# Low parts of keys and compressed probabilities as products over 128 partitions, and conditioning sums further down TensorE's list

## The chip, the cores and the metric

The kernel runs on one core of a Trainium2 chip. The metric is device time in microseconds (us) of one execution. Engines: PE is TensorE (products; PEld is its weight load), DVE is VectorE, ACT is ScalarE, POOL is GpSimd, SP is SyncE, which issues the DMAs here.

## What is computed

One decoder layer for 512 tokens of width 1024, in float32, with a conditioning vector `c`:

```
mod = (silu(c) @ w_ada + b_ada).reshape(9, 1024)            # shifts, scales, gates
x = x + 0.5 * gt1 * swiglu(modulate(rmsnorm(x, g1), sh1, sc1))
x = x + gt2 * mixer(modulate(rmsnorm(x, gm), sh2, sc2))
x = x + 0.5 * gt3 * swiglu(modulate(rmsnorm(x, g2), sh3, sc3))
out = rmsnorm(x, g_final)
```

The mixer projects its input once, into a gated depthwise convolution and into attention: 8 query heads of 64, in 2 groups that share keys and values. Each head has three branches, whose outputs are gated and added: over compressed blocks of keys (31 of them), over selected blocks, and over a window of 512. With 512 tokens the selected blocks and the window hold all earlier tokens. Both groups' outputs are normed and projected.

## The kernel before

Activations lie transposed, channels on partitions, tokens along the free axis. Products run in fp32r. To keep the precision of float32 an operand is split into a high part (rounded by ACT) and a low part (the difference, by DVE or POOL), and a product is made of three: `mm3` is high by high, high by low, low by high. Weights stream in units of 128x1024 (`raw`), are split into `whi` and `wlo`, and are freed when PE has used them.

The kernel is written as tasks (Python generators) that ask a planner (`Plan`) for an engine, with a cost in us. The planner places them in order of rank and of its own estimates of time; what comes out is one fixed list of instructions per engine. On the chip each engine follows its list in order and waits for what an instruction needs. `go(rank, task)` starts a task; `Slots` are buffers that tasks take and give back; `Event` is a point that tasks wait for. Names in the trace are those of the tiles: `b` is a PSUM bank, `hhi`, `hlo` the normed input, `ghi`, `glo` the gated values of the feed-forward part.

The order in time: the first feed-forward part with the first modulation (to some 410 us), beside which the other seven rows of `mod` are made; the mixer's first group of projections (to 470), the rest of the projections mixed with attention (to 665), the output projection, the second feed-forward part (from 706).

**Conditioning sums.** `ada_loads` brings `w_ada` in 56 loads of 512 KB through three buffers (`araw`); `ada_sums` adds eight of them, each scaled by its part of `silu(c)`, into `ada` on DVE (two such tiles). When the eighth is in, `ada_reduce` adds over partitions by PE (4 products with a matrix of ones), copies, transposes and adds the bias.

**Scores.** For head pair `c`, branch `b` (selected blocks, window) and group `s`, `scores` makes four tiles of 128 tokens by 128 to 512 keys, in three PSUM banks. Its `q` holds 128 rows: for group 0 the high part of the query in the lower 64 and the low part in the upper 64, for group 1 the other way round. `kst[b][s]` (in the trace `ks`) holds the high part of the keys in both halves, so that one product over 128 rows gives high by high and low by high. The third, the query's high part by the keys' low part, is a product over the 64 rows where the high part lies; `klo[b]` (`kl`) holds group 0 in its lower and group 1 in its upper half:

```
mm(a, q[:, tt], st[:, :w], True, False)
mm(a, q[hs, tt], lo[hs, :w], False, True)
```

The planner's cost for these is 2 * max(w / 2370, 0.105) us at a width of w. After that come the mask and a minimum (DVE, `P`), the exponential (ACT), a scaling, transposes on PE (line 1407), a split into `PT` and the products with the values (`values`: 128 columns of output for the high part of `PT`, 64 for its low part, in the same bank).

**Compressed branch.** `compressed` leaves the transposed probabilities as high part `pcs[0]` and low part `pcs[1]` of 64 rows (both groups' 32 blocks), and `values` ends each head with a product of 64 rows by 64 columns and one of 64 rows by 128 (`pc,vcs`). The upper half of that bank (the values' low parts) is copied to `low` and added later by `pair`.

Of the kernel before, what the change touches and what calls it, by code (L numbers as in the profile page):

```python
# [10 lines left out]
F32 = mybir.dt.float32  # L11
F32R = mybir.dt.float32r
BF16 = mybir.dt.bfloat16
I32 = mybir.dt.int32
AF = mybir.ActivationFunctionType
# [4 lines left out]
P = 128  # L20
T = 512
D = 1024
DK = D // P
# [4 lines left out]
HD = 64  # L28
# [45 lines left out]
A_ACT = 3  # L74
HOLD = 0
N_AW = 3
KEEP = (2, 2, 0)
N_PT = 4
R_H0 = 0.4
# [56 lines left out]
class Plan:  # L136
# [12 lines left out]
    def go(self, rank, task):  # L149
        self.n += 1  # L150
        self.step([rank, self.n, task, [self.at], None], None)
# [67 lines left out]
def c_act(n):  # L219
    return ACT, 0.1 + 0.84e-3 * n  # L220
# [18 lines left out]
def c_pts(n):  # L239
    return POOL, 0.26 + 0.83e-3 * n  # L240
# [15 lines left out]
def tile_hymba_layer(ctx: ExitStack, tc: tile.TileContext, xT, pos, cols_d, con_d, wa0, wa1, f1a, f1b, f1d,  # L256
                     wia, wib, wiv, wc1, woa, wob, f2a, f2b, f2d, out):
    nc = tc.nc
# [25 lines left out]
    def mm(o, lhsT, rhs, start, stop):  # L284
        nc.tensor.matmul(o, lhsT, rhs, start=start, stop=stop)  # L285
# [576 lines left out]
            done(aw_in[n])  # L862

    def ada_sums():
        for n in range(7 * DK):
            i, k = divmod(n, DK)
            yield aw_in[n]
            if k == 0:
                j = yield adas
            a, w = ada[j], aw[aw_at[n]]  # L870
            if k == 0:
                yield c_ts(D)
                nc.vector.tensor_scalar(a, w, cact[:, 0:1], None, op0=OP.mult)
            else:
                yield c_stt(D)
                nc.vector.scalar_tensor_tensor(a, w, cact[:, k:k + 1], a, op0=OP.mult, op1=OP.add)  # L876
            give(aws, aw_at[n])
            if k == DK - 1:
                go(R_ADA, ada_reduce(order[i], j))

    def ada_reduce(m, j):

# [90 lines left out]
    with ExitStack() as mixer:  # L973
# [6 lines left out]
        G = mx.tile([P, NB, 24], F32, name="G")  # L980
        valid = kv("valid").rearrange("p (t n) -> p t n", t=NB)
        vneg = mx.tile([P, NB, 32], F32, name="vneg")
        vcs = [mx.tile([64, P], F32R, name=f"vcs{g}") for g in range(2)]
        kcs = [mx.tile([P, 64], F32R, name=f"kcs{g}") for g in range(2)]
        ecmp = mx.tile([P, NB, 2, 32], F32, name="ecmp")
        kst = [[mx.tile([P, T], F32R, name=f"ks{b}{g}") for g in range(2)] for b in range(2)]
        klo = [mx.tile([P, T], F32R, name=f"kl{b}") for b in range(2)]
        q_of = [[mx.tile([P, T], F32R, name=f"q{i}{g}") for g in range(2)] for i in range(2)]
        p_of = [[mx.tile([P, (t + 1) * P], F32, name=f"P{i}{t}") for i in range(N_P[t])] for t in range(NB)]
        ps_ = [Slots(range(n)) for n in N_P]  # L990
# [13 lines left out]
        def constants():  # L1004
            for s_ in swp_of:
                yield c_pts(T)
                nc.gpsimd.memset(s_, 0.0)
            yield c_pts(P)
            nc.gpsimd.tensor_scalar(vneg, valid, 1.0, NEG, op0=OP.subtract, op1=OP.mult)
            yield c_pts(P)  # L1010
            for g in range(2):
                nc.gpsimd.memset(vcs[g].bitcast(F32), 0.0)
            for g in range(2):
                yield c_pts(64)
                nc.gpsimd.memset(kcs[g].bitcast(F32), 0.0)
            yield c_pts(64)
            nc.gpsimd.memset(blk[:, :, :, NC_CMP:], 0.0)
            done(ready0)
# [61 lines left out]
        def keys(b):  # L1080

            def then(o):
                for g, h in enumerate((LO_, HI_)):
                    for part in ((LO_, HI_) if g == 0 else (HI_, LO_)):
                        yield from copy(kst[b][g][part], o[h], T)
                    yield c_tt(T)
                    nc.vector.tensor_sub(klo[b][h], o[h], kst[b][g][h].bitcast(F32))
                done(k_in[b])
            return then

# [55 lines left out]
        def compressed_keys(bs):  # L1146
# [31 lines left out]
            for g in range(2):  # L1178
                r = slice(g * 32, (g + 1) * 32)
                yield ACT, 0.2  # L1180
                nc.scalar.activation(vcs[g][r, LO_], pt[r, :HD], AF.Copy)
                yield SMALL
                nc.vector.tensor_sub(vcs[g][r, HI_], pt[r, :HD], vcs[g][r, LO_].bitcast(F32))
            done(vc_in)
            side_free(ib)
            ib = yield from side_bank()
# [18 lines left out]
        def compressed(c):  # L1205
# [46 lines left out]
                nc.tensor.transpose(pt[:64, t * P:(t + 1) * P], e[:, t].rearrange("p a b -> p (a b)"), ident)  # L1252
            give(e_free, 0)
            yield c_act(T)
            nc.scalar.activation(pcs[0], pt[LO_], AF.Copy)
            yield c_tt(T)
            nc.vector.tensor_sub(pcs[1], pt[LO_], pcs[0].bitcast(F32))
            side_free(ib)
            done(pc_in[c])

        pc_turn = [Event() for _ in range(5)]
        e_free, pc_free = Slots([0]), Slots([0])
        pcs = [mx.tile([HD, T], F32R, name=f"pc{i}") for i in range(2)]

        low, lows = mx.tile([P, T], F32, name="low"), [Slots([0]), Slots([0])]
        pc_in, cq_done = [Event() for _ in range(4)], [Event() for _ in range(4)]
        z_in, z_of = [Event() for _ in range(8)], {}

# [47 lines left out]
        def scores(c, b, s, n_, order):  # L1316
# [1 line left out]
            yield begun[n_]  # L1318
            yield k_in[b]
            yield q_in[c]  # L1320
            hs = (LO_, HI_)[s]
            q, st, lo = q_of[q_at[c]][s], kst[b][s], klo[b]
            k = yield hsmall
            m, su = small_of[k][:, 0, :, 0], small_of[k][:, 1, :, 0]
            pi, left = None, [NB]
# [18 lines left out]
            for ts in ((3,), (2,), (1, 0)):  # L1344
                j = yield caps["s"]
                bk = yield banks
                if ts[-1] == 0:
                    done(begun[n_ + 1])
                yield PE, sum(2 * max((t + 1) * P / 2370, 0.105) for t in ts)
                at = 0  # L1350
                a_of = {}
                for t in ts:
                    w = (t + 1) * P
                    tt = slice(t * P, w)
                    a_of[t] = a = bank_of[bk][:, at:at + w]
                    at += w
                    mm(a, q[:, tt], st[:, :w], True, False)
                    mm(a, q[hs, tt], lo[hs, :w], False, True)
                n = [len(ts)]

                def free(n=n, j=j, bk=bk):
                    n[0] -= 1
                    if not n[0]:
                        give(caps["s"], j)
                        give(banks, bk)

                for t in ts:
                    go(order, softmax(t, a_of[t], free))
# [59 lines left out]
        def values(c, s):  # L1428
# [17 lines left out]
            yield pc_in[c]  # L1446
            yield vc_in
            yield PE, 0.43
            mm(o[LO_], vcs[s][:, LO_], pcs[1], False, False)
            mm(o, vcs[s], pcs[0], False, True)  # L1450
            summed[c] += 1
            if summed[c] == 2:
                give(pc_free, 0)
            yield lows[s]
            yield c_act(T)
            nc.scalar.activation(low[(LO_, HI_)[s]], o[HI_], AF.Copy)
            yield zp_open
            y = z_tile[4 + c]
            yield c_act(T)
            nc.scalar.activation(y[(LO_, HI_)[s]], o[LO_], AF.Copy)  # L1460
# [4 lines left out]
        def pair(c):  # L1465
            for s in range(2):
                yield attended[c][s]
            y = z_tile[4 + c]
            e = yield c_tt(T), (*c_ptt(T), POOL_TAX)
            (nc.vector if e == DVE else nc.gpsimd).tensor_add(y, y, low)  # L1470
            for s in range(2):
                give(lows[s], 0)
            yield from group_norm(y, cv("ga", c), 4 + c)

        summed = [0] * 4
        zp_open, z_tile = Event(), {0: mx.tile([P, T], F32, name="z0")}

        def free_queries(c):
# [147 lines left out]
        plan.run(early_done)  # L1626
        early.close()
        zp = mixer.enter_context(tc.tile_pool(name="zp", bufs=1))
        for k in range(1, 8):
            z_tile[k] = zp.tile([P, T], F32, name=f"z{k}")  # L1630
        for i in range(N_LATE_P):
# [272 lines left out]
```

## Time and profile before

| | us |
|---|---|
| median of 3 runs | 1070.98 (1069.9 to 1071.71) |
| the profiled execution | 1075.31 |
| its span in the trace | 1073.5 |
| PE busy | 1048.8 |
| DVE busy | 607.3 |
| ACT busy | 409.2 |
| POOL busy | 50.1 |

The trace is of one execution. An engine is busy while it runs an instruction; a matmul's end is modelled, and the next may start before it, so that PE's pace is better read from the starts of its products. The view of one stretch after another tells which engine is full where.

### The profile page before, as it was taken

Reading aid. Unit: us, or ns where it says so; the run is one execution under the profiler, and the core shown is the slowest. Engines: PE = TensorE matmul, PEld = TensorE weight load, DVE = VectorE, ACT = ScalarE, POOL = GpSimd, SP = SyncE. Lnnn points to the kernel's source line nnn. Section 1 sums busy time; section 2 is a strip of 40 time slices with the busy share of each in tenths; the row PEclk is TensorE's granted clock in tenths of the full one; section 3 lists DMA queues with packets and bytes.
Section 4 is the critical chain, followed back from the end, with each engine's and each line's share of the span. In section 5 each row is a group of like instructions: output and inputs, shape, how many; then the busy total and the mean of one; then the engine's idle time right before and its main releaser. Section 6 shows DMA issues by size and latency. Waiting matters only on the chain.

```text
span 1073.5 us, 13889 instructions
## 1 busy us (share of the span) xinstructions
PE 1048.8 (98%) x5417; PEld 865.9 (81%) x5417; DVE 607.3 (57%) x1069; ACT 409.2 (38%) x713; POOL 50.1 (5%) x47
## 2 busy tenths in 40 slices
PE   8899999999999999999999999999999999999997
PEld 5787777788888889987777677898888888888887
DVE  4978788833333347499788687664333333333334
ACT  4542222122222233347756685444222112222321
POOL 0310000000000001012001010100000000000000
PEclk8899999999999999999999899999999999999998
DMA  9659889522232230343300002314333322333302
GB/s 340 253 194 323 310 310 318 183 98 98 98 98 98 98 103 16 131 126 120 132 25 28 13 13 78 112 60 137 98 96 94 94 95 95 97 98 98 99 20 79
DMA packets 40707, 133.60 MB, mean 124 GB/s; under 512 B 4705, under 2 KB 8033, under 8 KB 40001
## 3 DMA queue, kind: packets, MB, share of 16 engines
q1 hardware_dynamic: 40640, 132.71, 36.7%
q8 instruction: 42, 0.69, 0.3%
q14 instruction: 25, 0.20, 0.1%
HBM read 130.14 MB, written 2.10 MB: 123 GB/s over the span
## 4 chain that ended last, share of the span: by engine, by line
PE 80%; DVE 9%; DMA 7%; issue 2%; ACT 1%; SPq 0%; DVEq 0%; ACTq 0%
PE b L285 77%; DMA araw<-in_wa_dram 6%; DVE ada L876 3%; PE b L1407 2%; DVE wlo L366 1%; DVE s L530 0%; ACT whi L377 0%; DVE afirst L747 0%; DMA raw<-in_f1b_dram 0%; DMA x<-in_xT_dram 0%; DVE s L611 0%; DVE glo L618 0%; PE b L1302 0%; DVE s L1050 0%; DVE swp L1053 0%
## 5 line engine op out<-in xcount | busy, mean ns | idle before, releaser
L285 PE MATMUL b<-hhi,whi 128*128 128x512 f32 (+1 forms) x1020 | 383.7, 376 | 1.1 <-ACT hhi L534 1.1
L285 PE MATMUL b<-hlo,whi 128*128 128x512 f32 (+1 forms) x1020 | 376.6, 369 | 0.7 <-DVE hlo L536 0.7
L285 PE MATMUL b<-hhi,wlo 128*128 128x512 f32 (+1 forms) x1020 | 376.5, 369 | 0.0
L377 ACT ACTIVATE whi<-raw 128x1024 fp32r<-128x1024 f32 (+3 forms) x176 | 178.0, 1012 | 445.0 <-PE b L285 300.7
L366 DVE TENSOR_TENSOR wlo<-raw,whi 128x1024 fp32r<-128x1024 f32 (+3 forms) x162 | 191.0, 1180 | 213.5 <-ACT whi L377 212.4
L285 PEld LDWEIGHTS b<-hhi,whi 128*128 128x128 f32 x1020 | 193.5, 190 | 38.9 <-issue 6.5
L285 PEld LDWEIGHTS b<-hhi,wlo 128*128 128x128 f32 x1020 | 193.6, 190 | 32.2
L285 PEld LDWEIGHTS b<-hlo,whi 128*128 128x128 f32 x1020 | 193.7, 190 | 30.4 <-DVE hlo L536 1.0
L285 PE MATMUL b<-ghi,whi 128*128 128x512 f32 (+1 forms) x364 | 136.4, 375 | 0.0
L285 PE MATMUL b<-ghi,wlo 128*128 128x512 f32 (+1 forms) x364 | 135.7, 373 | 0.0
L285 PE MATMUL b<-glo,whi 128*128 128x512 f32 (+1 forms) x364 | 135.7, 373 | 0.0
L611 DVE TENSOR_TENSOR s<-sg,b 128x512 f32<-128x512 f32 x44 | 30.1, 685 | 101.9 <-PE b L285 101.2
L285 PEld LDWEIGHTS b<-ghi,whi 128*128 128x128 f32 x364 | 68.5, 188 | 12.8 <-issue 0.8
L285 PEld LDWEIGHTS b<-ghi,wlo 128*128 128x128 f32 x364 | 68.5, 188 | 12.1
L285 PEld LDWEIGHTS b<-glo,whi 128*128 128x128 f32 x364 | 68.5, 188 | 12.0
L876 DVE SCALAR_TENSOR_TENSOR ada<-araw,cact,ada 128x1024 f32<-128x1024 f32 x49 | 66.6, 1360 | 18.9 <-DMA araw<-in_wa_dram 18.4
L543 DVE SCALAR_TENSOR_TENSOR x<-b,mod,x 128x512 f32<-128x512 f32 (+1 forms) x30 | 19.1, 643 | 41.0 <-PE b L285 40.9
L366 POOL TENSOR_TENSOR wlo<-raw,whi 128x768 fp32r<-128x768 f32 (+2 forms) x14 | 31.1, 2220 | 216.6 <-ACT whi L377 216.6
L461 ACT ACTIVATE s<-x 128x256 f32<-128x256 f32 (+1 forms) x41 | 19.4, 491 | 55.4 <-DVE x L543 53.6
L616 ACT ACTIVATE ghi<-s 128x512 fp32r<-128x512 f32 x44 | 27.5, 630 | 22.3 <-DVE s L611 22.3
L534 ACT ACTIVATE hhi<-s,mod 128x256 fp32r<-128x256 f32 (+1 forms) x42 | 20.9, 534 | 29.4 <-DVE s L530 26.3
L1416 ACT ACTIVATE PT<-b 128x384 fp32r<-128x384 f32 (+1 forms) x48 | 24.5, 524 | 17.9 <-PE b L1407 17.3
(238 smaller groups left out, 974.3 us busy)
## 6 DMA issues: line engine op xcount, KB each, us to landing
araw<-in_wa_dram SPq DMA_DIRECT2D x56, 512.0 KB
raw<-in_f1b_dram SPq DMA_DIRECT2D x38, 512.0 KB
raw<-in_f2b_dram SPq DMA_DIRECT2D x38, 512.0 KB
raw<-in_f1d_dram SPq DMA_DIRECT2D x22, 512.0 KB
raw<-in_f2d_dram SPq DMA_DIRECT2D x22, 512.0 KB
raw<-in_wib_dram SPq DMA_DIRECT2D x14, 512.0 KB
wfirst<-in_wa_dram SPq DMA_DIRECT2D x5, 1024.0 KB
raw<-in_wc_dram SPq DMA_DIRECT2D x8, 512.0 KB
```

Source lines behind the costliest of these rows:

```text
L285: nc.tensor.matmul(o, lhsT, rhs, start=start, stop=stop)
L366: (nc.vector if e == DVE else nc.gpsimd).tensor_sub(wlo_of[j][:, :n], raw_of[i][:, :n], whi_of[j][:, :n].bitcast(F32))
L377: nc.scalar.activation(whi_of[j][:, :n], raw_of[raw_at[u]][:, :n], AF.Copy)
L461: nc.scalar.activation(o[:, ts], x[d][:, ts], AF.Square)
L534: nc.scalar.activation(hhi[d][:, ts], t, AF.Identity, bias=sh)
L543: nc.vector.scalar_tensor_tensor(x[d][:, ts], bank_of[b][:, ts], gate, x[d][:, ts], op0=OP.mult, op1=OP.add)
L611: nc.vector.tensor_mul(scr_of[q], sg_of[k], bank_of[bu])
L616: nc.scalar.activation(ghi[j], scr_of[q], AF.Copy)
L876: nc.vector.scalar_tensor_tensor(a, w, cact[:, k:k + 1], a, op0=OP.mult, op1=OP.add)
L1407: nc.tensor.transpose(pt[:, w:w + P], Pr[t][:, kb * P:(kb + 1) * P], ident)
L1416: nc.scalar.activation(ph[:, :w], pt[:, :w], AF.Copy)
```

## The change

- `klo` gets a tile for each branch and group, as `kst` has. Its other half is set to zero by POOL when the mixer begins (four memsets of 64x512), and the product of the low part runs over all 128 rows of `q`: the zeros take the query's low part out.
- `pcs` becomes one tile of 128 rows, high part below, low part above. `vcs` gets 128 rows; ACT copies the values' high part a second time, beside the low part of `pcs`. One product over 128 rows takes the place of two over 64.
- `low` moves into the pool `zp`, which is opened later (`zp_open`); the wait for it stands ahead of the copy to `low` and no longer behind it.
- `ada_sums` calls `ada_reduce` when the fourth load of the next eight is added (`LATER = 3`), and no longer at once; the last of the seven at once, as before.

```
+LATER = 3
...
     def ada_sums():
+        summed = []
         for n in range(7 * DK):
...
             if k == DK - 1:
-                go(R_ADA, ada_reduce(order[i], j))
+                summed.append((order[i], j))
+            if summed and (k == LATER or n == 7 * DK - 1):
+                go(R_ADA, ada_reduce(*summed.pop()))
...
-        vcs = [mx.tile([64, P], F32R, name=f"vcs{g}") for g in range(2)]
+        vcs = [mx.tile([P, P], F32R, name=f"vcs{g}") for g in range(2)]
...
-        klo = [mx.tile([P, T], F32R, name=f"kl{b}") for b in range(2)]
+        klo = [[mx.tile([P, T], F32R, name=f"kl{b}{g}") for g in range(2)] for b in range(2)]
...
+            for b in range(2):
+                for g, other in enumerate((HI_, LO_)):
+                    yield c_pts(T)
+                    nc.gpsimd.memset(klo[b][g][other].bitcast(F32), 0.0)
...
-                    nc.vector.tensor_sub(klo[b][h], o[h], kst[b][g][h].bitcast(F32))
+                    nc.vector.tensor_sub(klo[b][g][h], o[h], kst[b][g][h].bitcast(F32))
...
+                yield ACT, 0.2
+                nc.scalar.activation(vcs[g][HD + g * 32:HD + (g + 1) * 32, LO_], pt[r, :HD], AF.Copy)
...
-            nc.scalar.activation(pcs[0], pt[LO_], AF.Copy)
+            nc.scalar.activation(pcs[LO_], pt[LO_], AF.Copy)
             yield c_tt(T)
-            nc.vector.tensor_sub(pcs[1], pt[LO_], pcs[0].bitcast(F32))
+            nc.vector.tensor_sub(pcs[HI_], pt[LO_], pcs[LO_].bitcast(F32))
...
-            hs = (LO_, HI_)[s]
-            q, st, lo = q_of[q_at[c]][s], kst[b][s], klo[b]
+            q, st, lo = q_of[q_at[c]][s], kst[b][s], klo[b][s]
...
-                    mm(a, q[hs, tt], lo[hs, :w], False, True)
+                    mm(a, q[:, tt], lo[:, :w], False, True)
...
-            mm(o[LO_], vcs[s][:, LO_], pcs[1], False, False)
-            mm(o, vcs[s], pcs[0], False, True)
+            mm(o, vcs[s], pcs, False, True)
...
             yield lows[s]
+            yield zp_open
             yield c_act(T)
-            nc.scalar.activation(low[(LO_, HI_)[s]], o[HI_], AF.Copy)
-            yield zp_open
+            nc.scalar.activation(low_of[0][(LO_, HI_)[s]], o[HI_], AF.Copy)
```

What the planner makes of it is seen in the engines' lists. PE, at the first of the seven sums over partitions (`ada,con`), before, among the projections of the first feed-forward part (rows 429 to 433 of its list):

```order
L285 MATMUL b_64<-hlo_121,whi_100 128x512
L285 MATMUL b_64<-hhi_113,wlo_101 128x512
L285 MATMUL b_70<-ada_663,con 32x256 x4
L285 MATMUL b_64<-hhi_114,whi_100 128x512
L285 MATMUL b_64<-hlo_122,whi_100 128x512
```

and the same sum now, at rows 465 to 469:

```order
L286 MATMUL b_65<-hlo_117,whi_96 128x512
L286 MATMUL b_65<-hhi_109,wlo_97 128x512
L286 MATMUL b_66<-ada_663,con 32x256 x4
L286 MATMUL b_65<-hhi_110,whi_96 128x512
L286 MATMUL b_65<-hlo_118,whi_96 128x512
```

It stands 36 rows further down. The other five of the first six move by 39 to 42 rows. PE at the last of the seven, before, rows 858 to 862:

```order
L285 MATMUL b_63<-glo_687,whi_96 128x512
L285 MATMUL b_63<-ghi_676,wlo_97 128x512
L285 MATMUL b_64<-ada_663,con 32x256 x4
L285 MATMUL b_63<-ghi_677,whi_96 128x512
L285 MATMUL b_63<-glo_688,whi_96 128x512
```

and now:

```order
L286 MATMUL b_69<-glo_687,whi_96 128x512
L286 MATMUL b_69<-ghi_676,wlo_97 128x512
L286 MATMUL b_63<-ada_663,con 32x256 x4
L286 MATMUL b_69<-ghi_677,whi_96 128x512
L286 MATMUL b_69<-glo_688,whi_96 128x512
```

It stands in the same row, 860, ahead of the same product. POOL's list, before, from the end of the first feed-forward part (the last low parts of its weights) to the mixer's first low part:

```order
L366 TENSOR_TENSOR wlo_95<-raw_89,whi_94 128x1024
L366 TENSOR_TENSOR wlo_101<-raw_92,whi_100 128x1024
L1007 MEMSET swp_2756 128x512
L1007 MEMSET swp_2757 128x512
L1009 TENSOR_SCALAR vneg<-con 128x128
L1012 MEMSET vcs_2733 64x128
L1012 MEMSET vcs_2734 64x128
L1015 MEMSET kcs_2735 128x64
L1015 MEMSET kcs_2736 128x64
L366 TENSOR_TENSOR wlo_97<-raw_92,whi_96 128x768
```

and now, to the end of the memsets of `kl`:

```order
L367 TENSOR_TENSOR wlo_95<-raw_89,whi_94 128x1024
L367 TENSOR_TENSOR wlo_97<-raw_90,whi_96 128x1024 x2
L367 TENSOR_TENSOR wlo_101<-raw_92,whi_100 128x1024
L1011 MEMSET swp_2758 128x512
L1011 MEMSET swp_2759 128x512
L1013 TENSOR_SCALAR vneg<-con 128x128
L1016 MEMSET vcs_2733 128x128
L1016 MEMSET vcs_2734 128x128
L1020 MEMSET kl_2742 64x512
L367 TENSOR_TENSOR wlo_97<-raw_92,whi_96 128x768
L1020 MEMSET kl_2743 64x512
L1020 MEMSET kl_2744 64x512
```

Two more low parts of weights stand on POOL in the first feed-forward part, one memset of `kl` ahead of the mixer's low part and three behind it. In all, POOL has four more low parts of 1024 columns and one more of 640, and DVE as many fewer; from the middle of the attention stage on, the order of the tasks differs in many places on every engine.

## Rows read from the trace of the kernel before

**Rows 1.** The page, busy us (share of the span) and instructions of each engine.

```profile
PE 1048.8 (98%) x5417; PEld 865.9 (81%) x5417; DVE 607.3 (57%) x1069; ACT 409.2 (38%) x713; POOL 50.1 (5%) x47
```

**Rows 2.** The page, chain that ended last, share of the span by engine.

```profile
PE 80%; DVE 9%; DMA 7%; issue 2%; ACT 1%; SPq 0%; DVEq 0%; ACTq 0%
```

**Rows 3.** Busy time by stretch (us from the span's start), instructions in brackets.

```profile
core 0: us, PE busy (x) PEld busy (x) DVE busy (x) ACT busy (x) POOL busy (x), PEclk, DMA share, GB/s
64.00:203.00 139.00, 129.89 (x603) 102.80 (x602) 111.79 (x114) 38.41 (x52) 4.96 (x2) 0.99 0.86 303
470.00:515.00 45.00, 44.75 (x233) 34.12 (x231) 43.64 (x87) 31.65 (x64) 6.30 (x3) 1.00 0.45 144
515.00:560.00 45.00, 45.00 (x242) 33.99 (x241) 36.20 (x93) 27.49 (x62) 3.54 (x3) 1.00 0.21 71
560.00:590.00 30.00, 30.00 (x146) 21.15 (x145) 24.68 (x81) 20.41 (x54) 3.86 (x4) 1.00 0.09 25
590.00:665.00 75.00, 74.67 (x402) 54.15 (x403) 55.76 (x186) 53.85 (x131) 5.91 (x9) 0.95 0.09 28
```

**Rows 4.** PE's products in order of time at 573 us: start, duration, what.

```profile
572.85 0.40 PE L285 MATMUL b<-ks,q 128*128 128x512 f32 x1
573.18 0.50 PE L285 MATMUL b<-kl,q 64*128 64x512 f32 x1
573.61 0.50 PE L285 MATMUL b<-hhi,whi 128*128 128x512 f32 x1
573.94 0.40 PE L285 MATMUL b<-hlo,whi 128*128 128x512 f32 x1
574.18 0.39 PE L285 MATMUL b<-hhi,wlo 128*128 128x512 f32 x1
```

**Rows 5.** The same at 582 us, four score products and a projection.

```profile
582.12 0.28 PE L285 MATMUL b<-ks,q 128*128 128x256 f32 x1
...
583.15 0.50 PE L285 MATMUL b<-hhi,whi 128*128 128x512 f32 x1
583.49 0.39 PE L285 MATMUL b<-hlo,whi 128*128 128x512 f32 x1
```

**Rows 6.** The same at 531 us, four products with values.

```profile
531.14 0.51 PE L285 MATMUL b<-PT,V 128*128 128x256 f32 x4
531.49 0.33 PE L285 MATMUL b<-ks,q 128*128 128x256 f32 x1
```

**Rows 7.** PE's products that read `kl`, by stretch.

```profile
470.00:515.00 45.00, 6.19 (x15) 1.00 0.45 144
515.00:560.00 45.00, 3.65 (x11) 1.00 0.21 71
560.00:590.00 30.00, 6.21 (x15) 1.00 0.09 25
590.00:665.00 75.00, 10.69 (x25) 0.95 0.09 28
```

**Rows 8.** PE in order of time at 588 us, the two compressed products.

```profile
587.88 0.68 PE L285 MATMUL b<-pc,vcs 64*64 64x512 f32 x2
588.49 0.44 PE L285 MATMUL b<-ks,q 128*128 128x384 f32 x1
```

**Rows 9.** PE at all sums (busy, mean ns, idle before), and at the last one.

```profile
L285 PE MATMUL b<-ada,con 128*32 128x256 f32 x56 | 4.5, 391 | 9.1 <-DVE ada L876 7.6 <-issue 1.5
...
200.87 0.64 PE L285 MATMUL b<-ada,con 128*32 128x256 f32 x8 [1.73 <-DVE ada L876]
```

**Rows 10.** DVE's groups from 64 to 203 us: busy, mean ns, idle before.

```profile
L876 DVE SCALAR_TENSOR_TENSOR ada<-araw,cact,ada 128x1024 f32<-128x1024 f32 x49 | 66.6, 1360 | 18.9 <-DMA araw<-in_wa_dram 18.4
L366 DVE TENSOR_TENSOR wlo<-raw,whi 128x1024 fp32r<-128x1024 f32 x21 | 25.6, 1218 | 2.8 <-ACT whi L377 2.8
```

**Rows 11.** POOL's groups from 411 to 665 us: busy, mean ns, idle before.

```profile
L366 POOL TENSOR_TENSOR wlo<-raw,whi 128x1024 fp32r<-128x1024 f32 x3 | 9.1, 3020 | 70.3 <-ACT whi L377 70.3
L1007 POOL MEMSET swp<- 128x512 f32 x2 | 1.0, 524 | 294.5 <-PE b L285 294.5
```

More of the change, by code (lines that the diff above doesn't have):

```diff
@@ L1262, in tile_hymba_layer @@
         e_free, pc_free = Slots([0]), Slots([0])
-        pcs = [mx.tile([HD, T], F32R, name=f"pc{i}") for i in range(2)]
-        low, lows = mx.tile([P, T], F32, name="low"), [Slots([0]), Slots([0])]
+        pcs = mx.tile([P, T], F32R, name="pc")
+        lows = [Slots([0]), Slots([0])]
         pc_in, cq_done = [Event() for _ in range(4)], [Event() for _ in range(4)]
@@ L1469, in pair @@
             e = yield c_tt(T), (*c_ptt(T), POOL_TAX)
-            (nc.vector if e == DVE else nc.gpsimd).tensor_add(y, y, low)
+            (nc.vector if e == DVE else nc.gpsimd).tensor_add(y, y, low_of[0])
             for s in range(2):
@@ L1475, in tile_hymba_layer @@
         summed = [0] * 4
+        low_of = []
         zp_open, z_tile = Event(), {0: mx.tile([P, T], F32, name="z0")}
@@ L1628, in tile_hymba_layer @@
         zp = mixer.enter_context(tc.tile_pool(name="zp", bufs=1))
+        low_of.append(zp.tile([P, T], F32, name="low"))
         for k in range(1, 8):
```

## The prediction

> **What bounds the kernel now.** I read the page's busy times first, then the chain that ended last, then busy times by stretch, then the starts of single products. TensorE (PE) is busy 98% of the span [rows 1] and holds 80% of the chain [rows 2]. Its ends are modelled, so I go by starts: a 128x512 product without a wait starts 0.23 us after the one before it [rows 4]. In the attention stage (470 to 665 us) PE is full in each stretch, while VectorE (DVE) is at 43.64 of 45, 36.20 of 45, 24.68 of 30 and 55.76 of 75 us [rows 3]. So whatever shortens PE's list there shortens the time, until DVE is full, which it already is before 515 us. From 64 to 203 us it is otherwise: there the DMA engines are 86% busy and DVE 80% [rows 3], and PE stands waiting for the conditioning sums.
>
> **Products over 128 partitions: low parts of keys.** Now each tile of scores is a product over 128 rows (`ks`) and one over 64 (`kl`). Around 573 us the starts are 572.85 (`ks`), 573.18 (`kl`), 573.61 and 573.94 (projection products) [rows 4]. The first three of them take 1.09 us; three products of this size without a `kl` take 3 x 0.23 = 0.69. So one 64-row product costs 0.40 us beside its work, part of it on the product ahead (0.33), most on its own (0.43), part on the one behind (0.33). The pairs of 256 and 128 columns agree: from 582.12 to 583.49 four such products and a projection product take 1.37 us [rows 5]; four products over 128 rows of the same sizes take 0.35 [rows 6], with the projection product 0.58. The excess is 0.79 for two, again 0.40 each. That it is the rows, and not the shared bank or the half-wide output, is what [rows 6] speak for: those four products share a bank too, and every second one has 64 columns of output. The 384-column pair I take at the same 0.40. With 64 such products: 64 x 0.40 = 25.6 us of PE time. The new products stream as many columns as the old, so nothing comes back.
>
> Here a rule of the Trainium skill speaks against the change: "TensorE: Matmul & The Clock Gate", section "Why this matters for your kernels", says that a single product over few rows takes as long as one over 128. By it alone the 64 products would keep their time and this part would give 0. Another page of the Trainium skill, "TensorEngine Tiling (Array Packing)", section "Key Properties", says that changing the tiling mode drains the array; by it the 0.40 us is the change of mode there and back, and goes. The rows side with the second for rows; for column tiles, which that page counts as modes too, they show no price.
>
> **Compressed values.** Two products over 64 rows become one over 128. The pair takes 587.88 to 588.49 = 0.61 us [rows 8]; with about 0.1 us each on the product ahead and behind, as in [rows 4], 0.81 against 0.23 for the one that stays: 0.58 x 8 = 4.6 us.
>
> **What of these 30.2 us comes through.** By stretch, `kl` products (two of the view's stand on a boundary and are counted twice: I use 15, 10, 14, 25 [rows 7]) and pairs of compressed values (0, 2, 1, 5 by where they start) give 6.0, 5.2, 6.2 and 12.9 us of relief. DVE does the masking, the low parts and the norms in its own fixed order, and none of that goes. The most that I see it do is 97% (43.64 of 45). At 97%, the stretches can shrink to 45.0, 37.3, 25.4 and 57.5 us: by 0, 7.7, 4.6 and 17.5. The smaller of relief and room: 0 + 5.2 + 4.6 + 12.9 = 22.7 us. At 85% the room would be 0, 2.4, 1.0 and 9.4, 12.8 us in all; with no limit from DVE it is the whole 30.2. I take 22.7, since the same order of work already runs DVE at 97% where DVE is behind. What is late next is then DVE's masking and low parts, behind whose results PE will wait for the first time in this stage.
>
> **Small additions.** Four more memsets on GpSimd (POOL), about 0.5 us each [rows 11], stand at the mixer's start, one of them ahead of a weight low part: 0.5 us late there, at most 2 if PE runs up against it; cover is the weights already made, I take 0. DVE first writes `kl` after the projections, behind all of them. Two more copies of 32x64 on ScalarE (ACT): ACT has 17 us of room before 560 us [rows 3]; 0. The buffer `low` is opened later, but the copy behind it waited for the same event; 0. The planner also gives POOL more low parts: 2 more full ones before the last sum, and in the mixer stage 2 full ones and one of 640 columns. Each takes 1.22 us from DVE [rows 10], but 3.0 on POOL instead [rows 11]; I count this only below.
>
> **Conditioning sums.** Seven times PE waits for a sum over eight loads; the view gives 9.1 us of idle [rows 9]. Six of the seven sums now stand 36 products or a few more later, 36 x 0.23 = 8.3 us. The last does not move: PE's row 860 in both. That decides. The sums' pace is a ring of DMA, DVE and buffers: DVE stands 18.9 us for loads and 2.8 us for the weights' high parts [rows 10]; PE is hardly in it. If the last sum is ready at 200.8 us as now, PE comes to it about 8 us sooner and waits 8 us longer than its present 1.73 [rows 9]: the waits are gathered in one place, not removed. What can come forward is the last sum itself: two low parts off DVE (2 x 1.22), up to 2.8 us of that wait; 0 to 5.2 us, and I take 1.5, because 18.9 us of DVE's idle time is for loads, which don't come sooner.
>
> **Sum.** 22.7 + 1.5 = 24.2 us. The profiled execution took 1075.31 us (span 1073.5 and 1.8 around it), so 1051.1 there; it is 4.3 us over the median of 1070.98, so 1046.8 as a median: 1047, with 1041 to 1054 as this case's own range. A measurement of this kernel can tell about 0.2% (2 us) from no change.
>
> **Rivals.**
> - *PE stays the bound.* DVE's order was planned with a cost of w/2370 us for each product of a pair, 0.22 at 512 columns, which is the price of a product over 128 rows and not of the present pair; so DVE may be able to follow the quicker PE throughout. Against it: 43.64 of 45 before 515 us. The whole 30.2 + 1.5: 1039.
> - *The wait for the sums goes away too.* If the ring does run through PE (ACT's high parts wait for buffers that PE frees), the last sum comes forward with PE and a further 6.7 us or more go: 1040 with the likeliest attention stage, 1032 with the first rival. Against it: DVE's 2.8 us.
> - *DVE stalls in its order.* With PE no longer late, softmax waits of DVE for ACT and POOL show, and POOL's low parts take 3.0 us; DVE reaches only 85%: 12.8 + 1.5, 1057.
> - *The rows have no price.* The excess comes from something else in the pair, and only eight products go: 8 x 0.23 = 1.8 us and at most 1.5 from the sums: 1068 to 1071. Against it: [rows 6].
> - *Slower: the clock.* PE waiting on DVE loses its clock: between 590 and 665 us the mean granted clock was 0.95 [rows 3], that is some 7 us at 1.2 instead of 2.4 GHz, at a loss of half of that. If the gain is 24.2 us, PE would have to spend over 48 us more at 1.2 GHz to end over 1071, three quarters of the 62 us left between 590 and 665; all of them would give 1047 + 31 = 1078. Before, no stretch of the stage has a clock under 0.95, so I hold it unlikely. The Trainium skill, "TensorE: Matmul & The Clock Gate", section "Why this matters for your kernels", warns of such drops where PE idles between products; no row here shows one from waits as short as these.
>
> **How the numbers follow.** Chances: the likeliest 0.52, PE stays the bound 0.14, the sums too 0.10, DVE stalls 0.17, no price 0.04, slower 0.03. Most of the second and third case and of the fourth are needed for 8 in 10: 1034 to 1060. Faster takes the first four and part of the fifth, 0.94; same 0.03; slower 0.03.
>
> **What would show it.** Right: every `kl` product runs over 128 rows and starts of its neighbours are 0.23 us apart at 512 columns; one `pc` product per head; DVE over 90% busy in the attention stage and PE idle there for DVE; the six moved sums without idle time, and 8 to 10 us of idle in front of the last, still ready near 200 us. Wrong: `kl` products still 0.3 us or more apart from their neighbours at 256 columns; the last sum ready 6 us sooner; or PE without a wait from 515 to 640 us, which would mean the first rival.

## The result, and the profile after

The changed kernel takes 1058.64 us (median of 4 runs, 1057.17 to 1059.17). The kernel before took 1071.35 us in four runs beside it. The ratio is 0.9888, with an interval of 0.987 to 0.9906: 12 us quicker, where 24 were forecast. The profiled execution took 1059.17 us, its span is 1057.4.

The page of the changed kernel, busy times and the chain by engine, which answer to [rows 1] and [rows 2]:

```profile
PE 1024.0 (97%) x5409; PEld 859.6 (81%) x5409; DVE 607.2 (57%) x1064; ACT 409.0 (39%) x719; POOL 62.7 (6%) x52
...
PE 73%; DVE 13%; DMA 9%; issue 2%; ACT 2%; SPq 0%; DVEq 0%; ACTq 0%
```

PE is busy 25 us less and holds 73% of the chain in place of 80%. Most of what it lost there went to DVE and the DMA engines.

Busy time by stretch of the changed kernel, columns as in [rows 3]:

```profile
64.00:203.00 139.00, 129.69 (x597) 101.97 (x596) 112.13 (x112) 37.80 (x52) 10.80 (x4) 0.97 0.86 301
470.00:515.00 45.00, 41.52 (x237) 34.79 (x236) 43.82 (x83) 30.61 (x60) 8.56 (x4) 1.00 0.45 145
515.00:560.00 45.00, 43.71 (x261) 35.46 (x259) 39.27 (x105) 32.40 (x78) 7.83 (x4) 1.00 0.24 82
560.00:590.00 30.00, 30.00 (x188) 25.22 (x188) 26.31 (x86) 24.63 (x63) 3.18 (x3) 1.00 0.09 26
590.00:665.00 75.00, 71.89 (x417) 57.62 (x417) 61.95 (x185) 55.13 (x128) 8.76 (x9) 1.00 0.19 61
```

PE was full in the attention stage and now has gaps. DVE, which the forecast took up to 97%, is there only before 515 us (43.82 of 45); later it is at 87, 88 and 83%. ACT is at 68 to 82%. After 515 us no engine but PE is nearly full, and yet PE waits.

PE's products in order of time, at two places of the changed kernel (start, duration, what), which answer to [rows 4] and [rows 5], and one of the single products of the compressed values, for [rows 8]:

```profile
538.62 0.39 PE L286 MATMUL b<-ks,q 128*128 128x512 f32 x1
538.85 0.40 PE L286 MATMUL b<-kl,q 128*128 128x512 f32 x1
539.08 0.39 PE L286 MATMUL b<-hhi,whi 128*128 128x512 f32 x1
539.31 0.39 PE L286 MATMUL b<-hlo,whi 128*128 128x512 f32 x1
...
569.48 0.28 PE L286 MATMUL b<-ks,q 128*128 128x256 f32 x1
...
569.78 0.27 PE L286 MATMUL b<-kl,q 128*128 128x128 f32 x1
569.89 0.45 PE L286 MATMUL b<-hhi,whi 128*128 128x512 f32 x1
570.18 0.40 PE L286 MATMUL b<-hlo,whi 128*128 128x512 f32 x1
...
577.54 0.44 PE L286 MATMUL b<-pc,vcs 128*128 128x512 f32 x1
577.82 0.34 PE L286 MATMUL b<-ks,q 128*128 128x384 f32 x1
```

At 512 columns three starts take 0.69 us, where they took 1.09: the excess of 0.40 is gone. In the group of 256 and 128 columns five products take 0.70 us in place of 1.37: 0.67 for two, not 0.79. The last `kl`, of 128 columns, takes 0.11 and the product behind it 0.29, where 0.06 and 0.23 had been reckoned; so this part of the excess belonged to short products and not to their rows. The compressed product takes 0.28 us, where the pair took 0.61. Its neighbours are quicker too, which is seen where they are products of 512 columns; before:

```profile
547.28 0.40 PE L285 MATMUL b<-hhi,wlo 128*128 128x512 f32 x1
547.61 0.67 PE L285 MATMUL b<-pc,vcs 64*64 64x512 f32 x2
```

and in the changed kernel:

```profile
547.01 0.40 PE L286 MATMUL b<-hhi,wlo 128*128 128x512 f32 x1
547.25 0.40 PE L286 MATMUL b<-pc,vcs 128*128 128x512 f32 x1
547.48 0.39 PE L286 MATMUL b<-hhi,whi 128*128 128x512 f32 x1
```

The product ahead holds PE for 0.33 us before and 0.24 now, and the compressed product itself is down to 0.23 here.

The sums: PE's two groups from 64 to 203 us (busy, mean ns, idle before), for [rows 9]:

```profile
L286 PE MATMUL b<-ada,con 128*32 128x256 f32 x56 | 4.9, 426 | 5.3 <-DVE ada L878 5.3
L899 PE MATMUL b<-con,s 128*128 128x128 f32 x12 | 2.3, 276 | 3.6 <-ACT s L896 3.6
```

Seven waits of 9.1 us in all have become two of 8.9: one of 3.6 us, in front of a sum's transposes at 115 us, and one of 5.3 in front of the last sum, whose products start at 200.91 us, as they did before at 200.87. PE in order of time around it, and below it the stretch's busy times and granted clock:

```profile
195.25 0.39 PE L286 MATMUL b<-ghi,wlo 128*128 128x512 f32 x1
200.91 1.08 PE L286 MATMUL b<-ada,con 128*32 128x256 f32 x8 [5.27 <-DVE ada L878]
...
203.79 0.63 PE L286 MATMUL b<-glo,whi 128*128 128x512 f32 x1
204.22 0.63 PE L286 MATMUL b<-ghi,wlo 128*128 128x512 f32 x1
```

```profile
198.00:205.00 7.00, 4.09 (x17) 2.62 (x17) 4.12 (x7) 0.38 (x1) 0.00 (x0) 0.51 0.42 153
```

The granted clock from 198 to 205 us is 0.51, the level of 1.2 GHz. It falls while PE stands idle, and when the sum is ready PE runs 4 us of products at 0.43 us each in place of 0.23. Behind the wait of 3.6 us at 115 us it is low as well: products start 0.43 us apart from 120 to 123 us:

```profile
121.00:123.00 2.00, 2.00 (x7) 1.52 (x6) 1.75 (x4) 0.00 (x0) 0.00 (x0) 0.50 0.87 283
```

### The profile page after: what moved, and what is told of

It is laid out like the page before. It is cut to its first block, busy times and chain, and to the rows that moved or that the text cites. A ratio compares the mean times of both kernels' runs of the same rounds, so it can differ in the third digit from the quotient of the medians.

```text
span 1057.4 us, 13873 instructions
## 1 busy us (share of the span) xinstructions
PE 1024.0 (97%) x5409; PEld 859.6 (81%) x5409; DVE 607.2 (57%) x1064; ACT 409.0 (39%) x719; POOL 62.7 (6%) x52
## 4 chain that ended last, share of the span: by engine, by line
PE 73%; DVE 13%; DMA 9%; issue 2%; ACT 2%; SPq 0%; DVEq 0%; ACTq 0%
PE b L286 71%; DMA araw<-in_wa_dram 8%; DVE ada L878 3%; DVE wlo L367 1%; DVE PT L1427 1%; PE b L1416 1%; DVE afirst L748 1%; DMA wfirst<-in_wa_dram 1%; DVE P L1344 1%; DVE s L531 1%; ACT whi L378 0%; DMA raw<-in_f1b_dram 0%; DVE q L1108 0%; DVE s L1058 0%; DVE s L612 0%
## 5 line engine op out<-in xcount | busy, mean ns | idle before, releaser
L367 DVE TENSOR_TENSOR wlo<-raw,whi 128x1024 fp32r<-128x1024 f32 (+3 forms) x157 | 185.4, 1181 | 213.9 <-ACT whi L378 212.8
L878 DVE SCALAR_TENSOR_TENSOR ada<-araw,cact,ada 128x1024 f32<-128x1024 f32 x49 | 69.6, 1420 | 20.0 <-DMA araw<-in_wa_dram 19.6
L286 PEld LDWEIGHTS b<-glo,whi 128*128 128x128 f32 x364 | 68.8, 189 | 12.8 <-DVE glo L619 0.8
L367 POOL TENSOR_TENSOR wlo<-raw,whi 128x1024 fp32r<-128x1024 f32 (+2 forms) x19 | 43.9, 2311 | 286.8 <-ACT whi L378 260.7
L1427 DVE TENSOR_TENSOR PT<-b,PT 128x384 fp32r<-128x384 f32 (+1 forms) x48 | 28.0, 595 | 3.8 <-ACT PT L1425 3.6
```

What stands on the lines that cost most here:

```text
L367: (nc.vector if e == DVE else nc.gpsimd).tensor_sub(wlo_of[j][:, :n], raw_of[i][:, :n], whi_of[j][:, :n].bitcast(F32))
L1427: nc.vector.tensor_sub(pl[:, :w], pt[:, :w], ph[:, :w].bitcast(F32))
```

## The experiments

**First theory.** The products give what their starts say; from 515 us on PE then waits for results of DVE and ACT that come late, though neither is full, and the moved sums lose time instead of giving some. Rivals: DVE alone is the bound; PE's list is badly ordered; or the excess is a price of each 64-row product and the time went elsewhere.

**The kernel before, once more.** No edit.

> The kernel before, unchanged, for a second trace. Theory: the first trace held a spell at 1.2 GHz between 607 and 613 us that ordinary executions don't have, and was about 3.5 us long for it; a new trace then takes some 1071 to 1072 us, with no spell at 1.2 GHz between 470 and 665 us, and the attention stage (first product with V's weights to the second feed-forward part's first ghi product) is about 367.5 us instead of 371.0. Rival: the spell belongs to the kernel; then it is there again, and the stage is 371 us.

One execution, 1073.66 us. Busy times of one stretch in it:

```profile
605.00:612.00 7.00, 7.00 (x24) 3.99 (x25) 2.95 (x14) 2.76 (x9) 0.16 (x1) 0.52 0.00 0
```

The low clock is there again, in a stretch in which PE is busy without a break. In the first trace it lay a little later, and it is what made the 0.95 in [rows 3]:

```profile
608.00:613.00 5.00, 5.00 (x20) 3.01 (x20) 1.35 (x6) 1.68 (x7) 0.00 (x0) 0.50 0.00 0
```

The rival was right for this execution. But the run with copies on ScalarE added to the kernel before, below, has 1.00 there, as have those of the sums alone and with reductions on VectorE:

```profile
605.00:612.00 7.00, 7.00 (x39) 4.61 (x38) 5.24 (x24) 5.92 (x19) 0.48 (x1) 1.00 0.00 0
```

From the first `wlo,hhi` product (the values' projection, at some 450 us) to the first `ghi` product of the second feed-forward part (at some 820 us) both traces of the kernel before take 371.0 us and the later run 368.3; the run of the sums alone, whose edit lies outside this part, takes 368.1. The trace of before thus has 2.7 us there that are no price of the products, and for differences between traces the later run stands in its place. The first trace also has a low clock in the first feed-forward part, behind a wait for a sum of 1.98 us at 143 us:

```profile
146.00:149.00 3.00, 3.00 (x12) 2.28 (x9) 2.41 (x4) 0.90 (x2) 0.00 (x0) 0.50 0.92 355
```

The second has one at 127 us, behind a wait of 2.20 us. Both traced executions are some 4 us longer than the median of the kernel before.

**The sums alone.** The kernel before, with the changed `ada_sums`:

```
+            if summed and (k == LATER or n == 7 * DK - 1):
+                go(R_ADA, ada_reduce(*summed.pop()))
```

> The kernel before with LATER = 3 alone: six of the seven conditioning sums 36 products later, no other edit. Theory (the sums' pace is a ring of DMA and DVE, PE is not in it): PE's waits are gathered in front of the last sum, which stays at 200 to 201 us; the wait of 5 us or more there is followed by a spell at 1.2 GHz that costs 1.5 to 2.5 us: 1072.5 to 1074. Rival 1 (neutral, only the attention stage counts): 1071 to 1071.5. Rival 2 (the waits go): 1063 to 1066.

1073.7 us, ratio 1.004 (1.0026 to 1.0053): slower, as expected. The move costs some 4 us by itself. Its trace has the low clock twice, behind a wait of 5.9 us in front of the last sum and behind one of 2.7 us in front of a sum's transposes at 118 us; the expectation had only the first.

**The products alone.** The changed kernel, with the sums at once:

```
-            if summed and (k == LATER or n == 7 * DK - 1):
+            if summed:
```

> The changed kernel with the sums where they were before: products over 128 rows alone. Theory: without the wait and the spell at 1.2 GHz in front of and behind the last sum it is 1.5 to 2.5 us quicker than the changed kernel: 1056 to 1057.2. Rival 1 (the sums are neutral): 1058 to 1059.5. Rival 2 (the sums' edit brings part of the gain): 1061 or more.

1055.21 us, ratio 0.9864 (0.985 to 0.9879), against 1069.73 for the kernel before beside it. The products gain 14.5 us; 22.7 were forecast. Without the moved sums the kernel is 3 us quicker than the changed one; it lies 0.8 us below the range expected.

**The last sum moved too.** The changed kernel, with the last sum held back by 16 planned us, which puts it 75 rows further down PE's list:

```
-                go(R_ADA, ada_reduce(*summed.pop()))
+                go(R_ADA, ada_reduce(*summed.pop(), LAST * (n == 7 * DK - 1)))
```

> The changed kernel with the last sum moved down as well, by 75 rows (72 products, 16 us), so that no sum stands in PE's way. Theory (PE is outside the ring and weights are ready ahead): PE passes 200 us without waiting, the wait of 5.3 us, the 2 us of slow clock and part of the 3.6 us at 115 us are gained: 1048 to 1053. Rival (PE then waits as long for the low parts of weights, which DVE makes at the ring's pace): 1057 to 1059.5.

1052.78 us, ratio 0.9841 (0.9827 to 0.9854). The wait in front of the last sum is gone, and so is the fallen clock behind it. The wait at 115 us stays, with the low clock behind it. In the changed kernel's trace one sees what makes it (all engines in order of time, rows between left out):

```profile
115.11 2.60 DVE L878 SCALAR_TENSOR_TENSOR ada<-araw,cact,ada 128x1024 f32<-128x1024 f32 x2 [2.51 <-DMA araw<-in_wa_dram]
...
117.63 0.68 DVE L612 TENSOR_TENSOR s<-sg,b 128x512 f32<-128x512 f32 x1
...
118.34 0.63 ACT L617 ACTIVATE ghi<-s 128x512 fp32r<-128x512 f32 x1 [5.27 <-DVE s L612]
118.88 0.37 ACT L896 ACTIVATE s<-b 128x256 f32<-128x256 f32 x1
119.30 0.44 PE L899 MATMUL b<-con,s 128*128 128x128 f32 x2 [3.63 <-ACT s L896]
```

DVE waits for a load; `s` stands behind these additions on DVE, `ghi` waits for `s` on ACT, the sum's copy stands behind `ghi`, and PE waits for the copy. The ring of loads reaches PE through the order of two other engines.

**Transposes moved too.** The run before, with the sum's transposes held back by 8 planned us behind their copy:

```
             nc.scalar.activation(t[:, :256], pc[:, :256], AF.Copy)
+            yield from wait(TURN)
             yield PE, 0.22
```

> The kernel after the change with the last sum moved down TensorE's list as in the run before (1052.8 us), and each sum's transposes 8 planned us further down, behind the copy that they read. Theory: the wait of some 4 us at 115 us in front of the transposes of a sum, and what stands behind it, goes, and nothing takes its place: 1047 to 1050. Rival: the loads' ring sets the pace of the sums, the wait moves to the next product that needs a sum or a buffer: 1052 to 1053.5.

1049.93 us (1047.24 to 1051.97), ratio 0.9811 (0.9795 to 0.9828), the upper end of what was expected. The wait at 115 us is gone, but smaller ones turn up from 168.50 us on; the granted clock from 166 to 172 us is 1.00:

```profile
168.50 0.49 PE L288 MATMUL b<-ghi,whi 128*128 128x512 f32 x1 [2.11 <-ACT ghi L619]
```

Of the waits for sums, most could be removed after all, once nothing of a sum stood early in PE's list.

**Two 64-row products side by side.** The kernel before, with `kl` ahead of `ks` in the tile of 128 columns:

```
+                    first = t == 0
+                    if first:
+                        mm(a, q[hs, tt], lo[hs, :w], True, False)
+                    mm(a, q[:, tt], st[:, :w], not first, first)
+                    if not first:
+                        mm(a, q[hs, tt], lo[hs, :w], False, True)
```

> The kernel before, with one swap: in the 128-column tile of the last bank of each head the product over 64 rows comes first and the one over 128 rows second, so that the two 64-row products of 256 and 128 columns stand side by side: 16 changes of the number of rows there and back fewer, as many products of 64 rows as before. Theory (the price lies in changing the number of rows and back): 16 x 0.40 = 6.4 us less, 1063 to 1065, and VectorE may let only part of it through, then 1065 to 1067. Rival (each 64-row product costs more, wherever it stands): no change, 1069 to 1071.

1066.48 us, ratio 0.996 (0.9946 to 0.9974), 3 to 6 us less, within what was expected if only a part comes through. PE in order of time in it:

```profile
578.50 0.28 PE L285 MATMUL b<-ks,q 128*128 128x256 f32 x1
578.71 0.44 PE L285 MATMUL b<-kl,q 64*128 64x256 f32 x2
579.08 0.33 PE L285 MATMUL b<-ks,q 128*128 128x128 f32 x1
579.24 0.44 PE L285 MATMUL b<-hhi,whi 128*128 128x512 f32 x1
579.52 0.39 PE L285 MATMUL b<-hlo,whi 128*128 128x512 f32 x1
```

The five products take 1.02 us, against 1.37 in [rows 5], with as many rows, columns and products: 0.35 less for one change of rows and back, 16 x 0.35 = 5.6 us on PE. The price is that of the change between 64 and 128 rows. Of the two rules of the Trainium skill in the prediction, the trace bears out that of "TensorEngine Tiling (Array Packing)", section "Key Properties" (changing the mode drains the array); the page gives no price, and here it is 0.34 to 0.40 us there and back.

**The compressed values alone.** The kernel before, with the edits of `vcs` and `pcs` and nothing else:

```
-            mm(o[LO_], vcs[s][:, LO_], pcs[1], False, False)
-            mm(o, vcs[s], pcs[0], False, True)
+            mm(o, vcs[s], pcs, False, True)
```

> The kernel before (some 1069.8 us) with the compressed values alone changed: one product over 128 rows in place of two over 64 in each of the 8 heads, the low parts of keys and the sums as before. By the prediction's term of 8 x 0.58 = 4.6 us: 1065 to 1066. By the trace of the changed kernel, in which the pairs gave 2.5 us on their own starts and perhaps 0.1 us each on a neighbour, 3.3 us at most, and less where VectorE lets less through: 1066.5 to 1068. Rival, no price of the rows here: 8 x 0.23 = 1.8 us, 1068.

1069.06 us against 1071.51, ratio 0.9977 (0.9964 to 0.999): 1 to 4 us less, 2.5 at the middle. The interval reaches to the rival's 1.8 us and does not quite reach the forecast's 4.6. The time alone thus does not tell the two apart; that the pair had a price is seen in the starts above. Of what PE's list lost, not all came through here either: from 450 to 700 us PE waits 1.9 us in this trace, where the run of the sums alone has 0.5.

**Work added on VectorE.** 16 reductions of 0.68 us, in the kernel with the products alone and in the kernel before:

```
+                if t == 3:
+                    nc.vector.tensor_reduce(spent, kv("mask"), axis=AX.X, op=OP.min)
```

> The kernel with the new products and the sums as before (the run of the new products alone took 1055.2 us), and one more reduction of 128x512 values on VectorE in each of the 16 heads' tiles of the last bank, whose result nothing uses. One of 128x256 takes 0.41 us in the profile, so some 0.6 to 0.7 us each is an estimate, 10 us of VectorE time in all. Theory: after the change VectorE's order holds TensorE back in the attention stage, so most of this comes through: 1061 to 1065. Rival: TensorE's own list is still the limit and the waits that it has there come from the chain through ScalarE and the score banks, with room for VectorE beside it: at most 3 us more, up to 1058.

> The same 16 reductions on VectorE in the kernel before (some 1069.7 us). Theory: there TensorE is the limit and VectorE has idle time in every stretch behind 515 us, so little comes through: 1 to 4 us, 1071 to 1074. Rival, that VectorE is as near the limit before the change as behind it: 6 us or more, 1076 and over.

With the new products 1061.04 us, ratio 0.9918 (0.9906 to 0.993), by the ratios 5.8 us over that of the products alone. That is the lower end of the theory's range, and half of the added 10.9 us, not most of it. In the kernel before 1071.45, ratio 1.0015 (1.0003 to 1.0026), 1.6 us. The added work is in both; in the first it reads:

```profile
L1349 DVE TENSOR_REDUCE spent<-con 128x1 f32<-128x512 f32 x16 | 10.9, 680 | 0.0
```

**Work added on ScalarE.** 48 copies of 0.31 us, at the same heads in the same two kernels:

```
+                if t == 3:
+                    for i in range(3):
+                        nc.scalar.activation(spent, kv("mask", i * P, P), AF.Copy)
```

> The kernel with the new products and the sums as before (1055.2 us), and three copies of 128x128 values on ScalarE, of some 0.27 us each, behind the exponentials of the last bank in each of the 16 heads: 13 us of ScalarE time whose result nothing uses. 16 reductions on VectorE of 10.9 us in all cost 5.8 us at the same place. Theory (VectorE in particular is what holds TensorE back, ScalarE has room): at most 3 us more, 1055 to 1058. Rival (the chain of products, VectorE and ScalarE holds it back as a whole, each link as much as the other): 5 us or more, 1060 and over.

> The three added copies on ScalarE in each of the 16 heads, in the kernel before. In the kernel with the new products they cost 5.2 us, against the theory that only VectorE holds it back. If TensorE is the limit before the change, and both other engines have slack there: 0 to 2 us more, 1.000 to 1.002 of before, as the reductions on VectorE gave 1.0015. Rival: ScalarE's copies stand in the chain of a head's softmax whatever TensorE does, and cost as much as there: 4 to 6 us, 1.004 to 1.006.

With the new products 1063.03 us against 1071.51, ratio 0.9912 (0.9899 to 0.9926): by the ratios 5.1 us over the products alone. My theory of VectorE in particular fell; the rival was right. In the kernel before 1070.18 against 1070.91, ratio 0.9997 (0.9985 to 1.001): nothing. PE's waits from 450 to 700 us in the kernel with products and copies (waiting line, what it waited for, us in total, times, longest), the two largest:

```profile
PE b L1294 <- ACT s L1292: 3.2, 2, 2.3
PE b L286 <- ACT s L1285: 2.5, 3, 1.4
```

and, as a comparison, all of them in the kernel before with the copies:

```profile
PE b L285 <- DVE PT L1422: 0.3, 1, 0.3
PE b L285 <- DVE wlo L366: 0.2, 1, 0.2
PE b L1284 <- ACT s L1282: 0.2, 1, 0.2
```

Before the change PE was late enough to hide 15 us of ACT's time and most of 11 us of DVE's. After it, about half of what is added on DVE, and a third on ACT, comes through. Up to 1.7 of ACT's 5.1 us may be clock: behind its wait of 2.3 us the granted clock of 494 to 498 us is 0.85 and of 498 to 502 us 0.73, together 3.4 us at the lower level.

**The group norms moved.** The best kernel so far, with the products that sum the squares and the transpose behind them held back by 1.5 planned us:

```
             nc.scalar.activation(q, y, AF.Square)
+            yield from wait(HOLD)
...
             nc.scalar.activation(q[:, :P], pc[:, :P], AF.Copy)
+            yield from wait(HOLD)
```

> The kernel with the sums' transposes moved too (0.981 of before), and in the group norms of the attention stage the products that sum the squares, and the transpose of these sums, 1.5 planned us further down TensorE's list or more. In the trace of the run without it TensorE waits 1.0, 1.6, 1.4 and 0.9 us at four such places for a copy or a square on ScalarE that runs late. Theory (the hold-back is the order of TensorE's list, whose head is not ready while products behind it are): some 3 to 5 us less, 0.977 to 0.978 of before. Rival (the chain through VectorE and ScalarE is late as a whole, as the runs with work added on either engine say): the waits turn up at other products, and the time stays within 1 us, 0.980 to 0.982.

1048.92 us, ratio 0.9802 (0.9778 to 0.9826): at the middle within 1 us of the run without it, as the rival said; the interval just reaches the theory's 0.978. The waits at the norms are gone and stand elsewhere (same view and stretch, the two largest):

```profile
PE b L1436 <- POOL P L1413: 2.9, 1, 2.9
PE b L1436 <- DVE vh L1364: 1.7, 1, 1.7
```

Both cost clock as well, as a window behind each shows (columns as in [rows 3]):

```profile
492.00:496.00 4.00, 4.00 (x27) 4.00 (x26) 3.30 (x7) 3.33 (x7) 0.00 (x0) 0.72 0.25 83
...
590.00:593.00 3.00, 3.00 (x13) 2.59 (x13) 2.56 (x11) 2.64 (x9) 0.14 (x1) 0.50 0.06 25
```

The run without this move has 1.00 throughout from 411 to 700 us. Some 6 us of products at the lower level cost up to 3 us, about what the theory had hoped to gain, so that this run does not tell the order of the list from the lateness of the chain. One move of this size doesn't recover the time; whether another order would is open.

## Why the prediction was wrong

**What bounds the kernel: right.** Taking 20 to 25 us off PE's list shortened the time, and before the change neither DVE nor ACT mattered much, as the added work shows.

**Low parts of keys, 64 x 0.40 = 25.6: a little too large.** The mechanism, a price for the rows that goes with them, was right. The 32 products of 512 and 384 columns give 0.40 each, if those of 384 do as those of 512; the 32 of 256 and 128 give 0.67 / 2. An estimate of the whole: 32 x 0.40 + 32 x 0.335 = 23.5 us. The 0.35 us of the group were taken as what four products of these sizes cost at best; with a `kl` of 128 columns last they cost more.

**Compressed values, 4.6: a little too large.** On its own starts a pair gives 0.61 - 0.28 = 0.33 us, and the neighbours give some 0.15 more (0.09 ahead; behind, a start 0.06 earlier among short products). An estimate for eight: 3.8 us. The 0.1 us for each neighbour, taken over from another pair, was nearly right; what was too low were the 0.23 us for the product that stays, which takes 0.28 where it follows short products. Timed alone, 2.5 us of this came through.

**What comes through, 22.7: the step that failed.** The runs show 14.5, and the traces 16.1 in the part named above (368.3 to 352.2), of which 0.9 is lost again in a wait at the mixer's start (1.2 us for `v`, where it was 0.3). The step was "at 97%": one stretch in which DVE was at 97% was taken as what the same order could reach everywhere. With the shares that DVE in fact has after 515 us, 87, 88 and 83%, the same rule gives room for 3.4, 2.0 and 7.8 us, 13.2 in all, close to 14.5. These shares are a result, not a cause. The cause, as far as the runs show it, is that PE now waits for single late results of DVE and ACT. From 450 to 700 us the changed kernel has 7.6 us of such waits, of which the four largest are:

```profile
PE b L286 <- ACT s L1284: 2.1, 2, 1.3
PE b L1293 <- ACT s L1291: 1.5, 1, 1.5
PE b L286 <- DVE pc L1267: 1.3, 1, 1.3
PE b L286 <- DVE wlo L367: 1.0, 2, 0.8
```

It is the rival "DVE stalls in its order" (12.8 us at 85%), but not for DVE's sake alone: copies on ACT cost 5.1 us at the same place. Summed over the starts of all of PE's products in this part (the run of the products alone against that of the sums alone), the score products, the compressed ones and the two groups beside them, `PT,V` and `hhi,whi`, take 25.5 us less; the two sizes above give 27.3 as an estimate. All other products take 9.7 us more, 7.3 of it in waits that the view names. With the 0.9 at the mixer's start this accounts for the 14.5 to within half a us. Some 2.4 us, most at transposes, are named by no view; a part may lie in modelled ends, which hide short waits.

**Small additions, 0: not measured apart.** The run of the products alone contains them too. PE waits 0.2 us for a low part on POOL in the changed kernel; whether the 0.9 us at the mixer's start belong here is open.

**Conditioning sums, +1.5: wrong in sign.** That the waits would be gathered and the last sum stay where it was came out to 0.04 us. One part of the waiting moved to a place that was not foreseen, the transposes of a sum, whose copy stands on ACT behind DVE's additions; in all PE waits as long as before (8.9 us against 9.1). The cost that was left out is the clock: the wait of 5.3 us is followed by 4 us of products at 1.2 GHz, 2 us lost, and the wait of 3.6 us by 3.4 us of them, 1.7 lost. Together, 3.7 us, that is about what the sums cost, 3 us here (1058.64 against 1055.21) and 4 in the kernel before. In the run of the products alone the clock is 1.00 from 64 to 203 us. All four runs of the changed kernel have a mean granted clock of 0.988 or 0.989, those of the products alone 0.990 to 0.992. The rival that the waits go away needed more than the change did: when the last sum and the transposes were moved too, 8 to 9 us came back against the changed kernel (1058.64 to 1049.93, or 0.9888 to 0.9811).

So 24.2 became 12: 8.2 less from the products, 4.9 less from the sums (14.5 - 3.4 = 11.1 by these medians). The loss of clock that I had as a rival happened, but at the sums and not in the attention stage, where PE's waits of up to 1.5 us left the clock at 1.00. No row of the prediction showed a drop from short waits; the trace that it was read from holds one, behind the wait of 1.98 us shown above. Here the warning of the Trainium skill, "TensorE: Matmul & The Clock Gate", section "Why this matters for your kernels", agrees with the trace for the waits of 3.6 and 5.3 us.

## What to carry to other kernels

When work is taken off a full engine, ask not how full the others can be but how early their results are: those that were hidden before by the full engine's lateness now end waits, on each engine that feeds it; a little work added on one of them before the change is no test, but on the changed kernel shows it at once. A product that runs on fewer rows than its neighbours pays for the change, not for itself, so put such products side by side if they can't be widened. Gathering waits removes nothing, and the long waits that come of it can cost clock on top; move the last consumer as well.

## What the runs showed of the hardware

The change between 64 and 128 rows costs 0.34 to 0.40 us there and back among fp32r products, on the product ahead, its own start and the one behind. The granted clock fell to half with the waits of 3.6 and 5.3 us of the changed kernel, and some 3 us of products ran at the lower level behind waits of 2.3 and 2.9 us in two runs. For shorter waits the traces here show both: it fell behind one of 1.7 us at 587 us of the last run and one of 2.0 us at 143 us of the first trace of the kernel before, and it stayed at 1.00 behind one of 2.1 us at 168 us of the run with the transposes moved, one of 2.6 us at 144 us of the run with products and copies, and all of up to 1.6 us from 64 to 700 us. It also fell to half for some 7 us at 605 to 607 us in both profiled executions of the kernel before, with PE busy throughout; in the runs of the sums alone, with reductions and with copies added to that kernel it did not, and no run here tells why.
